# Zeros ahead of the first matmuls, held first loads, and a free place for the third weight chunk in a two-layer decoder trunk

## The chip, the cores and the metric

The kernel runs on one core of one Trainium2 chip. The time is device microseconds of one execution of the whole program. In three runs the kernel before took 571.51 to 573.66 us, median 572.7 us.

## What is computed

A trunk of two decoder layers over 256 tokens of width 1024, all in float32. Layer 0 mixes tokens with a gated MLP over chunks of 128 positions, layer 1 with causal attention over 16 heads. Each layer then has a gated MLP of width 2816 with a causal convolution of width 3. Every sub-layer ends in a layer norm of `alpha * x + f(x)`. The change touches the first product of all, the `v` half of `x @ w_in`:

```python
def chunked_gmlp(x, w_in, ln_g, ln_b, w_s, b_s, w_out):
    z = jax.nn.gelu(x @ w_in)
    u, v = jnp.split(z, 2, axis=-1)
    v = layer_norm(v, ln_g, ln_b)
    ...
    sv = jnp.einsum('gts,bnsgc->bntgc', w, v) + b_s.T[None, None, :, :, None]
    return (u * sv.reshape(B, S, GMLP_WIDTH)) @ w_out

def reference(x, ...):
    for i in range(DEPTH):
        ...
        x = layer_norm(DN_ALPHA * x + y, ln_mix_g[i], ln_mix_b[i])
        y = conv_ffn(x, f_w_up[i], f_conv_w[i], f_conv_b[i], f_w_down[i])
        x = layer_norm(DN_ALPHA * x + y, ln_ffn_g[i], ln_ffn_b[i])
    return x
```

## The kernel before

**Products in three parts.** Each float32 operand is split into a rounded part (`hi`, type float32r) and the rest (`lo`), and a product is the sum of three TensorE products, hi·hi, hi·lo and lo·hi. `split` (L357) makes the two parts: the hi copy on ScalarE through `act` (L338) or on VectorE (L361), the lo subtraction on VectorE through `tt` (L344). All matmuls are issued by `mms` (L326), all loads by `load` (L355) on SyncE's queue.

**The weight stream.** All weights come as a stream of chunks of 128 x 2048 values, 1 MiB each (`stream`, L367). `prep(i)` (L385) loads chunk i into one of two `raw` tiles and splits it into two `sub` pairs of 128 x 1024, taken from a ring of ten `whi` and ten `wlo` tiles (five chunks). Chunks 0 to 4 are prepared at the start, each later one when the chunk five before it is used up (`spent`, L409). A `raw` tile is free again when both subs of its chunk have been split, so chunk 2 shares its tile with chunk 0 and chunk 3 with chunk 1.

**The order.** Operations are recorded first, with a cost each, and `Plan.emit` then gives every engine a fixed order by those costs and by due times. The nine first loads have a fixed rank instead, called load 0 to load 8 here: load 0 is columns 0 to 511 of chunk 0, load 2 columns 512 to 1023, load 4 columns 1024 to 2047 (`FIRST`, L382); load 6 and load 7 are the halves of chunk 1; loads 1, 3, 5 and 8 bring the transposed input `xT` for k = 0, k = 1, k = 2 and 3, and k = 4 to 7 (`XFIRST`, L383). After them SyncE's queue holds chunk 2, chunk 3, the layer norm's rows (`lnrow`), chunks 4 and 5, `wsT`, `bs`, and later ones.

**The first product** (`gmlp`, L641). Four PSUM banks hold the sums of two halves of the tokens (t = 0, 1) by two halves of the 1024 columns. Chunk c carries the rows of k = 2c (its first sub) and k = 2c + 1 (its second). A step (k, t) is six matmuls of 128 x 512, three for each column half (`rows_step`, L553). The order is k = 0 to 3 with both t, then k = 4 to 7 for t = 0, then k = 4 to 7 for t = 1: 16 steps, 96 matmuls. Within a column half the order is hi·hi, then input hi by weight lo, then input lo by weight hi. After it come GELU, layer norm and the `u` half (chunks 4 to 7).

**Space.** `ff` is a tile of 6144 columns whose parts are handed out by `place` (L251). At the start `xT` lies in columns 512 to 2559; columns 2560 to 4607 are idle until `wsT` (from 3072), `bs` (from 4096) and parts of `u` are placed there.

Of the kernel before, what the change touches and what calls it, by code (L numbers as in the profile page):

```python
# [18 lines left out]
P = 128  # L19
D = 1024  # L20
# [25 lines left out]
T1_WAITS = (2600, 3300, 4000, 4700)  # L46
REST = 25000, 9000, 25000
AHEAD = 12000


class Buf:
# [172 lines left out]
def trunk_kernel(ctx: ExitStack, tc: tile.TileContext, a: dict, out: bass.AP):  # L224
# [48 lines left out]
    banks += [b[:, o:o + HALF] for o in (0, HALF) for b in twos]  # L273
    ALONE, BY_TWO = range(BANKS // 2), range(BANKS // 2, BANKS)
    bank_of = [(i - BANKS, None, False) for i in range(BANKS)]
    state = {"age": 0, "next": 0}

    def taken(i, long):
        old = bank_of[i][1]
# [34 lines left out]
                bank_of[i] = (bank_of[i][0], b, False)  # L314


    def mms(seq, r, w, fill=False):

        ns = 0.0
        for o, l, x, _, _ in seq:  # L320
            n = flat(x)
            ns += max(107.0, n / 2.4) + 2.5 if l.dtype == F32R else (218.0 if n <= P else n / 0.6 + 5)

        def emit():
            for o, l, x, start, stop in seq:
                nc.tensor.matmul(o, l, x, start=start, stop=stop)  # L326
        plan.op("pe", ns, emit, r, w, fill)

# [21 lines left out]
    def ts(o, x, s1, s2, op0, op1, r, w):  # L350
        dve(187 + 0.52 * flat(x), lambda: nc.vector.tensor_scalar(o, x, s1, s2, op0=op0, op1=op1), r, w)

    def load(o, src, w, r=(), nbytes=None, rank=None):
        nbytes = nbytes or flat(o) * P * 4
        plan.op("sp", nbytes / 360.0, lambda: nc.sync.dma_start(o, src), r, w, nbytes=nbytes, rank=rank)  # L355

    def split(hi, lo, src, psum=False, by="act"):  # L357

# [21 lines left out]


    FIRST = {0: [(0, 512, 0), (512, 1024, 2), (1024, 2048, 4)], 1: [(0, 1024, 6), (1024, 2048, 7)]}  # L382
    XFIRST = ((0, 1, 1), (1, 1, 3), (2, 2, 5), (4, 4, 8))  # L383

    def prep(i):  # L385
        name, c = stream[i]
        raw = raws.new()
        cuts = FIRST.get(i, [(0, CH, None)])
        for s, e, rank in cuts:
            load(raw.ap[:, s:e], a[name][c, :, s:e], [(raw, range(s // 256, e // 256))], rank=rank)  # L390
        subs = []
        for s in range(2):
            hi, lo = whi.new(), wlo.new()
            pieces = [(0, 512), (512, 1024)] if i in FIRST or i in FINE else [(0, SUB)]
            for b, e in pieces:
                src = raw.ap[:, s * SUB + b:s * SUB + e]
                split((hi, range(b // 256, e // 256), hi.ap[:, b:e]), (lo, range(b // 256, e // 256), lo.ap[:, b:e]),
                      (raw, range((s * SUB + b) // 256, (s * SUB + e) // 256), src))
            subs.append((hi, lo))
        chunks[i] = subs  # L400
# [27 lines left out]

    xh, xl = xt_new()
    xT32 = place("ff", HALF, KT * S)  # L430
    xv32 = xT32.ap.rearrange("p (t k c) -> p t k c", t=NT, k=KT)

    def load_xt(k, n, rank):
        load(xv32[:, :, k:k + n, :], a["xT"][:, :, k:k + n, :], [(xT32, [(t, j) for t in range(NT) for j in range(k, k + n)])],
             rank=rank)
        for t in range(NT):
            parts = [(t, j) for j in range(k, k + n)]
            split((xh, parts, xt_view(xh)[:, t, k:k + n, :]), (xl, parts, xt_view(xl)[:, t, k:k + n, :]),
                  (xT32, parts, xv32[:, t, k:k + n, :]), by="dve" if k == 0 else "act")
# [9 lines left out]
    def ln_rows(i):  # L449
        b = rowring.new()  # L450
        src = a["lnrow"]
        load(b.ap, bass.AP(tensor=src.tensor, offset=src.offset + i * 2 * D, ap=[[0, P], [1, 2 * D]]), [b])
        return b, b.ap.rearrange("p (a d) -> p a d", a=2)

    def load_mixer():
# [94 lines left out]
            plan.later(wait, lambda k0=k0: turn(k0))  # L550


    def rows_step(pieces, hk, lk, r, hi, lo, first, last):  # L553

        for o, n, b in pieces:
            parts = range(o // 256, (o + n) // 256)
            mms([(b.ap[:, :n], x, w.ap[:, o:o + n], first and j == 0, last and j == 2)
                 for j, (x, w) in enumerate([(hk, hi), (hk, lo), (lk, hi)])], r + [(hi, parts), (lo, parts)], [b])
        plan.tick()

    def cols_times(b, h, l, hi, lo):
# [79 lines left out]
    def gmlp():  # L641
        at = xt_at(xh, xl)
        pieces = [[(o, HALF, bank(True)) for o in (0, HALF)] for _ in range(NT)]
        order = [(k, t) for k in range(4) for t in range(NT)] + [(k, t) for t in range(NT) for k in range(4, KT)]
        v = []
        for k, t in order:
            rows_step(pieces[t], *at(k, t), *sub("a_v", k // 2, k % 2), k == 0, k == KT - 1)
            if t == NT - 1 and k % 2:
                spent("a_v", k // 2)
            if (k, t) == (3, NT - 1):  # L650
                rows = ln_rows(0)
                ws, bs = load_mixer()
            if k == KT - 1:
                vt = place("ff", HALF + t * D, D)
                for o, n, b in pieces[t]:
                    act(vt.ap[:, o:o + n], b.ap, AF.Gelu_apprx_tanh, [b], [(vt, range(o // S, (o + n) // S))],
                        psum=True, table="gelu")
                    done_with(b)
                st, mean, rstd = stats(vt, vt.ap, [(0, HALF), (HALF, HALF)])
                scaled(vt, vt.ap, st, mean, rstd, rows)  # L660
                v.append(vt)
# [226 lines left out]
    at = conv_up(1, h, l)  # L888
    project_out("f_dn1", FT, at, xtok, None, 4)
    plan.tick(1e9)  # L890
    plan.emit()


# [9 lines left out]
def _layout(i):  # L903
# [10 lines left out]
    def paired(wa, wb):  # L914
# [3 lines left out]
    w_in, qkv = np.asarray(i["a_w_in"])[0], np.asarray(i["b_w_qkv"])[0]  # L918
    g = {
        "x": f(x.reshape(NT, P, D).transpose(1, 0, 2)),  # L920
        "xT": f(x.reshape(NT, P, KT, P).transpose(3, 0, 2, 1)),
        "a_v": by_rows(w_in[:, D:]),
        "a_u": f(tiles(w_in[:, :D]).reshape(4, 2, P, SUB).transpose(0, 2, 1, 3).reshape(4, P, CH)),
        "a_out": by_rows(np.asarray(i["a_w_out"])[0]),
# [45 lines left out]
```

## Time and profile before

| what | value |
|---|---|
| median of three runs | 572.7 us (571.51 to 573.66) |
| the profiled execution | 571.2 us |
| its span, first to last instruction | 569.5 us |
| mean granted TensorE clock | 0.995 |
| moved by DMA | 110.92 MB, mean 195 GB/s |

The span stands 1.7 us below the profiled execution's own time and 3.2 us below the median of the three runs. PE is TensorE's matmuls, PEld its weight loads, DVE VectorE, ACT ScalarE, POOL GpSimd, and SPq SyncE's queue, which issues the loads; L and a number is a line of the kernel. In a row of the timeline the first number is the start in us, the second the time that the group took, and the bracket the idle time of the engine before it, with what ended it.

### The profile page before, as it was taken

To read this page: it belongs to the slowest core of one execution; us is meant where nothing else is said; L and a number is where in the kernel's file an instruction comes from. 1 tells how busy PE (TensorE), PEld (TensorE's weight loads), DVE (VectorE), ACT (ScalarE), POOL (GpSimd) and SP (SyncE) were. 2 spreads that over 40 slices of the span, in tenths; PEclk is the share of its full clock that TensorE was granted. 3 is DMA by queue.
4 is the path that set the end of the run, shared out by engine and by line. 5 is a ranking of instruction groups with operands and counts; after the bars stand their busy time and mean duration, and the time that the engine had idled before them with its cause. 6 is when DMAs were issued, how large, how long until landed. Compare 5 with 4: busy or idle time off the path is not lost.

```text
span 569.5 us, 8289 instructions
## 1 busy us (share of the span) xinstructions
PE 556.1 (98%) x3098; PEld 474.9 (83%) x3098; DVE 464.3 (82%) x873; ACT 359.2 (63%) x652; POOL 11.5 (2%) x17
## 2 busy tenths in 40 slices
PE   6999999999999999999999999999999999999994
PEld 4799888888888878888888877788888888888884
DVE  5598989999999997467958988579989999996526
ACT  5555558776777686335578877377777767775300
POOL 0020010000000000001000000010000000000001
PEclk9999999999999999999999999999999999999998
DMA  7897435547554577742665653506455556566302
GB/s 266 330 361 283 181 146 182 189 153 279 171 211 155 216 229 266 270 165 74 222 221 185 194 210 115 222 2 221 156 218 219 201 174 218 195 242 229 147 1 74
DMA packets 20132, 110.92 MB, mean 195 GB/s; under 512 B 2251, under 2 KB 6268, under 8 KB 7676
## 3 DMA queue, kind: packets, MB, share of 16 engines
q1 hardware_dynamic: 20092, 110.39, 54.2%
q8 instruction: 24, 0.39, 0.3%
q14 instruction: 16, 0.13, 0.1%
HBM read 109.31 MB, written 1.07 MB: 194 GB/s over the span
## 4 chain that ended last, share of the span: by engine, by line
PE 95%; DMA 2%; DVE 1%; SPq 0%; ACT 0%; issue 0%; DVEq 0%
PE twos L326 52%; PE bank L326 41%; DMA raw<-in_a_v 2%; PE bank L332 1%; PE twos L332 1%; DVE wlo L344 0%; DVE x L348 0%; SPq L355 0%; ACT whi L338 0%; DVE stat L494 0%; DVEq L966 0%; DVE stat L497 0%; DVE stat L499 0%; DVE xt L344 0%
## 5 line engine op out<-in xcount | busy, mean ns | idle before, releaser
L344 DVE TENSOR_TENSOR wlo<-raw,whi 128x1024 fp32r<-128x1024 f32 (+1 forms) x212 | 228.2, 1099 | 33.7 <-ACT whi L338 32.8
L338 ACT ACTIVATE whi<-raw 128x1024 fp32r<-128x1024 f32 (+1 forms) x212 | 194.8, 954 | 55.1 <-DMA raw<-in_f_dn 21.3
L326 PE MATMUL twos<-xt,whi 128*128 128x512 f32 x640 | 222.2, 394 | 0.0
L326 PE MATMUL twos<-xt,wlo 128*128 128x256 f32 x640 | 177.3, 277 | 0.0
L326 PEld LDWEIGHTS twos<-xt,whi 128*128 128x128 f32 x640 | 120.0, 188 | 27.8
L326 PE MATMUL bank<-whi,rr 128*128 128x512 f32 x432 | 135.5, 391 | 0.0
L326 PEld LDWEIGHTS twos<-xt,wlo 128*128 128x128 f32 x640 | 120.1, 188 | 0.1
L326 PEld LDWEIGHTS bank<-whi,rr 128*128 128x128 f32 x432 | 81.1, 188 | 17.9 <-issue 1.0
L326 PE MATMUL bank<-wlo,rr 128*128 128x512 f32 x216 | 84.0, 389 | 0.0
L326 PE MATMUL bank<-xt,whi 128*128 128x256 f32 (+1 forms) x256 | 71.0, 348 | 0.0
L348 DVE SCALAR_TENSOR_TENSOR ff<-ff,convc 128x254 f32<-128x254 f32 (+1 forms) x160 | 69.6, 478 | 0.3
L338 ACT ACTIVATE ff<-twos 128x512 f32<-128x512 f32 (+1 forms) x56 | 30.8, 565 | 47.9 <-PE twos L326 44.8
L326 PE MATMUL bank<-xt,wlo 128*128 128x256 f32 x192 | 54.0, 281 | 0.0
L326 PEld LDWEIGHTS bank<-xt,whi 128*128 128x128 f32 x256 | 44.0, 190 | 6.8 <-issue 1.0
L326 PEld LDWEIGHTS bank<-wlo,rr 128*128 128x128 f32 x216 | 40.6, 188 | 8.0
L338 ACT ACTIVATE ff<-ff,convc 128x256 f32<-128x256 f32 x80 | 45.6, 592 | 1.9 <-DVE ff L344 1.2
L344 DVE TENSOR_TENSOR ff<-twos,ff 128x512 f32<-128x512 f32 (+1 forms) x48 | 30.9, 645 | 15.3 <-ACT ff L338 13.0
L326 PE MATMUL twos<-whi,xt 128*128 128x512 f32 x128 | 42.1, 396 | 0.0
L338 ACT ACTIVATE ff<-bank,lncol 128x128 f32<-128x128 f32 x48 | 18.8, 458 | 29.1 <-PE bank L332 29.1
L326 PEld LDWEIGHTS bank<-xt,wlo 128*128 128x128 f32 x192 | 36.4, 190 | 0.0
L348 DVE SCALAR_TENSOR_TENSOR x<-x,bank 128x512 f32<-128x512 f32 x16 | 11.0, 686 | 25.0 <-PE bank L326 25.0
L326 PEld LDWEIGHTS twos<-whi,xt 128*128 128x128 f32 x128 | 24.1, 188 | 4.8
(71 smaller groups left out, 489.1 us busy)
## 6 DMA issues: line engine op xcount, KB each, us to landing
raw<-in_f_up SPq DMA_DIRECT2D x44, 1024.0 KB, 4.8
raw<-in_f_dn SPq DMA_DIRECT2D x22, 1024.0 KB, 4.9
raw<-in_b_qk SPq DMA_DIRECT2D x8, 1024.0 KB, 4.9
lnrow<-in_lnrow SPq DMA_DIRECT2D x5, 1024.0 KB, 6.7
raw<-in_a_u SPq DMA_DIRECT2D x4, 1024.0 KB, 5.1
raw<-in_a_out SPq DMA_DIRECT2D x4, 1024.0 KB, 5.0
raw<-in_b_v SPq DMA_DIRECT2D x4, 1024.0 KB, 4.9
raw<-in_b_o SPq DMA_DIRECT2D x4, 1024.0 KB, 5.0
```

Source lines behind the costliest of these rows:

```text
L326: nc.tensor.matmul(o, l, x, start=start, stop=stop)
L332: nc.tensor.transpose(o, x, ident.ap)
L338: plan.op("act", ns, lambda: nc.scalar.activation(o, x, func, **kw), r, w, table=table)
L344: dve(70 + 1.04 * flat(x), lambda: nc.vector.tensor_tensor(o, x, y, op=op), r, w)
L348: lambda: nc.vector.scalar_tensor_tensor(o, x, s, y, op0=op0, op1=op1), r, w)
```

## The change

Five edits, all at the start of the program; the costs given to the planner stay as they are.

- Before everything that the planner ordered, VectorE sets 512 columns of the still unused tile `rr` to zero, and TensorE does eight matmuls of 128 x 512 on them into the last PSUM bank.
- Some loads are preceded on SyncE's queue by a transfer of 16 numbers that reads a place of an earlier chunk and so waits until that part of it has landed. Load 5 is so held by load 0, load 7 by load 4, the halves of chunk 2 by loads 6 and 7, the halves of chunk 3 by the halves of chunk 2, and the first `lnrow` by the first half of chunk 3.
- Chunk 2 goes to columns 2560 to 4607 of `ff`. Chunk 3 then takes the `raw` tile of chunk 0, chunk 4 that of chunk 1, and the later ones alternate as before. Chunks 2 and 3 are each loaded in two halves.
- `xT` lies in the order k, t, so that a load of n values of k is one run of n x 1024 bytes in each partition, where it was two runs of n x 512.
- The twelve matmuls of k = 0 are issued together, for each column half in the order hi·hi for both t, input lo by weight hi for both t, input hi by weight lo for both t.

```diff
+WARM = 8
...
-    def mms(seq, r, w, fill=False):
+    def mms(seq, r, w, fill=False, into=None, ready=False):
...
         def emit():
-            for o, l, x, start, stop in seq:
+            if into is not None and not ready:
+                return
+
+            for o, l, x, start, stop in seq if into is None else [q for _, _, q in sorted(into, key=lambda q: q[:2])]:
                 nc.tensor.matmul(o, l, x, start=start, stop=stop)
...
-    def load(o, src, w, r=(), nbytes=None, rank=None):
+    def load(o, src, w, r=(), nbytes=None, rank=None, holds=()):
...
+        n = flat(o) // max(1, len(holds))
+
+        def emit():
+            for j, (i, at) in enumerate(holds):
+                k = state["held"] = state["held"] + 16
+                nc.sync.dma_start(scratch[:, k:k + 16], loaded[i].ap[:1, at:at + 16])
+                if len(holds) > 1:
+                    nc.sync.dma_start(o[:, j * n:(j + 1) * n], src[:, j * n:(j + 1) * n])
+            if len(holds) < 2:
+                nc.sync.dma_start(o, src)
...
+    HOLD = {5: [(0, 0)], 7: [(0, SUB)], (2, 0): [(1, 0), (1, SUB)], (3, 0): [(2, 0), (2, SUB)]}
+    scratch = sb.tile([1, 128], F32, name="scratch")
+    loaded = {}
+    EARLY = 2
...
-        raw = raws.new()
+        raw = loaded[i] = raws.new()
+        if i == EARLY:
+
+            other = place("ff", HALF + KT * S, CH)
+            raw.ap, raw.prev = other.ap, raw.prev + other.prev
+            owners["ff"] = [(s, e, raw if b is other else b) for s, e, b in owners["ff"]]
+        elif i > EARLY:
+            raw.ap = raws.tiles[(i - 1) % RAWS]
...
-            load(raw.ap[:, s:e], a[name][c, :, s:e], [(raw, range(s // 256, e // 256))], rank=rank)
+            load(raw.ap[:, s:e], a[name][c, :, s:e], [(raw, range(s // 256, e // 256))], rank=rank,
+                 holds=HOLD.get(rank if rank is not None else (i, s), ()))
...
-    xv32 = xT32.ap.rearrange("p (t k c) -> p t k c", t=NT, k=KT)
+    xv32 = xT32.ap.rearrange("p (k t c) -> p t k c", t=NT, k=KT)
...
-        load(xv32[:, :, k:k + n, :], a["xT"][:, :, k:k + n, :], [(xT32, [(t, j) for t in range(NT) for j in range(k, k + n)])],
-             rank=rank)
+        sl = slice(k * S, (k + n) * S)
+        load(xT32.ap[:, sl], a["xT"][:, sl], [(xT32, [(t, j) for t in range(NT) for j in range(k, k + n)])], rank=rank,
+             holds=HOLD.get(rank, ()))
...
-        load(b.ap, bass.AP(tensor=src.tensor, offset=src.offset + i * 2 * D, ap=[[0, P], [1, 2 * D]]), [b])
+        load(b.ap, bass.AP(tensor=src.tensor, offset=src.offset + i * 2 * D, ap=[[0, P], [1, 2 * D]]), [b],
+             holds=[(3, 0)] if i == 0 else ())
...
-    def rows_step(pieces, hk, lk, r, hi, lo, first, last):
-
-        for o, n, b in pieces:
+    def rows_step(pieces, hk, lk, r, hi, lo, first, last, into=None):
+
+
+        for i, (o, n, b) in enumerate(pieces):
             parts = range(o // 256, (o + n) // 256)
-            mms([(b.ap[:, :n], x, w.ap[:, o:o + n], first and j == 0, last and j == 2)
-                 for j, (x, w) in enumerate([(hk, hi), (hk, lo), (lk, hi)])], r + [(hi, parts), (lo, parts)], [b])
+            seq = [(b.ap[:, :n], x, w.ap[:, o:o + n], first and j == 0, last and j == 2)
+                   for j, (x, w) in enumerate([(hk, hi), (hk, lo), (lk, hi)])]
+            if into is not None:
+                into += [(i, (0, 2, 1)[j], q) for j, q in enumerate(seq)]
+            mms(seq, r + [(hi, parts), (lo, parts)], [b], into=into, ready=into is not None and len(into) == 12)
         plan.tick()
...
+        into = []
         for k, t in order:
-            rows_step(pieces[t], *at(k, t), *sub("a_v", k // 2, k % 2), k == 0, k == KT - 1)
+            rows_step(pieces[t], *at(k, t), *sub("a_v", k // 2, k % 2), k == 0, k == KT - 1, into if k == 0 else None)
...
     plan.tick(1e9)
+
+    zeros = rr[:, :HALF]
+    nc.vector.memset(zeros.bitcast(F32), 0.0)
+    for _ in range(WARM):
+        nc.tensor.matmul(banks[-1], zeros[:, :P], zeros, start=True, stop=True)
     plan.emit()
...
-        "xT": f(x.reshape(NT, P, KT, P).transpose(3, 0, 2, 1)),
+        "xT": f(x.reshape(NT, P, KT, P).transpose(3, 2, 0, 1).reshape(P, KT * S)),
```

More of the change, by code (lines that the diff above doesn't have):

```diff
@@ L275, in trunk_kernel @@
     bank_of = [(i - BANKS, None, False) for i in range(BANKS)]
-    state = {"age": 0, "next": 0}
+    state = {"age": 0, "held": -16}
     def taken(i, long):
@@ L351, in ts @@
         dve(187 + 0.52 * flat(x), lambda: nc.vector.tensor_scalar(o, x, s1, s2, op0=op0, op1=op1), r, w)
-    def load(o, src, w, r=(), nbytes=None, rank=None):
+    def load(o, src, w, r=(), nbytes=None, rank=None, holds=()):
         nbytes = nbytes or flat(o) * P * 4
-        plan.op("sp", nbytes / 360.0, lambda: nc.sync.dma_start(o, src), r, w, nbytes=nbytes, rank=rank)
+        n = flat(o) // max(1, len(holds))
[7 more added lines that the diff above has]
+                nc.sync.dma_start(o, src)
+        plan.op("sp", nbytes / 360.0, emit, r, w, nbytes=nbytes, rank=rank)
     def split(hi, lo, src, psum=False, by="act"):
```

## The prediction, made before the changed kernel was run

> **What bounds the kernel now.** I began with the page's busy times and the chain that ended last:
>
> ```profile
> PE 556.1 (98%) x3098; PEld 474.9 (83%) x3098; DVE 464.3 (82%) x873; ACT 359.2 (63%) x652; POOL 11.5 (2%) x17
> ...
> PE 95%; DMA 2%; DVE 1%; SPq 0%; ACT 0%; issue 0%; DVEq 0%
> ```
>
> TensorE's matmuls carry 95% of the chain, so only time in which TensorE waits or runs slowly can go. The view of waits, asked for TensorE's matmuls over the whole span, has two rows:
>
> ```profile
> PE bank L326 <- DVE xt L361: 4.9, 1, 4.9
> PE bank L326 <- DVE wlo L344: 0.8, 1, 0.8
> ```
>
> Both belong to the first product. The chain in order of time shows what lies behind them:
>
> ```profile
> 3.15 5.63 DMA raw<-in_a_v
> 8.80 0.64 ACT whi L338
> ...
> 10.79 7.21 DMA raw<-in_a_v
> 18.03 1.07 ACT whi L338
> 19.12 1.24 DVE wlo L344
> 20.40 19.62 PE bank L326 x119
> ```
>
> Load 4 lands at 8.78. Its splits free raw tile 0, chunk 2 is issued at 10.79 and lands at 18.00, its splits take to 20.4, and from there the chain stays on TensorE. So I cut the first product into three windows (the columns are the stretch, its length, PE busy with matmuls counted, PEld busy likewise, granted clock, DMA share and GB/s) and looked at its matmuls in the timeline:
>
> ```profile
> 4.92:11.03 6.11, 6.03 (x14) 4.39 (x14) 1.00 0.90 308
> 11.03:20.40 9.37, 8.61 (x37) 6.57 (x36) 1.00 0.99 370
> 20.40:31.23 10.83, 10.83 (x48) 8.93 (x48) 1.00 0.87 323
> ...
> 4.92 0.77 PE L326 MATMUL bank<-whi,xt 128*128 128x512 f32 x1 [4.92 <-DVE xt L361]
> 5.77 0.80 PE L326 MATMUL bank<-wlo,xt 128*128 128x512 f32 x1
> ...
> 7.22 0.63 PE L326 MATMUL bank<-wlo,xt 128*128 128x512 f32 x1
> ...
> 8.50 0.63 PE L326 MATMUL bank<-wlo,xt 128*128 128x512 f32 x1
> ...
> 11.03 0.40 PE L326 MATMUL bank<-wlo,xt 128*128 128x512 f32 x1
> 11.26 0.40 PE L326 MATMUL bank<-whi,xt 128*128 128x512 f32 x1
> ```
>
> A window also counts the matmul that reaches into it, so 13, 36 and 47 start in the three, 96 in all. The last take 10.83 / 47 = 0.23 us each; between 7.22 and 8.50 three start, 0.43 each. The granted clock column reads 1.00 throughout, so the half rate, which ends at 11.03, shows in the spacing alone. At 0.23 the 96 would take 22.1 us, and they take 31.23 - 4.92 = 26.3. **These 4.2 us are all there is to gain** after the first matmul: 6.1 - 13 x 0.23 = 3.1 before 11.03, and 9.4 - 36 x 0.23 = 1.1 around the wait for chunk 2. The edits do nothing to the first load or its split, so the start stays.
>
> **The change part by part.** First the zeros and the new order of k = 0:
>
> ```profile
> 0.87 0.06 DVE L421 MEMSET nhalf<- 128x1 f32 x1 [0.87 <-PEq L963]
> ...
> 5.03 0.68 DVE L344 TENSOR_TENSOR wlo<-raw,whi 128x512 fp32r<-128x512 f32 x1
> 5.63 0.29 DVE L344 TENSOR_TENSOR xt<-ff,xt 128x128 fp32r<-128x128 f32 x1
> ```
>
> The memset of 128x512 has no row; it lies between 0.06 (one column) and 0.68 (a subtraction of its size). I take 0.4, since a fill reads nothing. It starts at 0.87, where VectorE has no other work until the input lands. Eight matmuls at 0.43 then run from 1.3 to 4.7, with a first latency of 0.77 to 5.0. They cost the path 0.1 us at most.
>
> What they buy: the rate rose 6.1 us after the first matmul, or 5.3 after the unbroken run from 5.77. Counted from 1.3, that is 6.6 to 7.4; I take 7.0. The new order starts with four matmuls that need no weight lo part (ready at 5.71), so the hole from 5.35 to 5.77 goes. From 5.0, five matmuls at 0.43 and seven at 0.23 end k = 0 at 8.8, against some 10.2 (12 matmuls) before. By "TensorE: Matmul & The Clock Gate" of the Trainium skill (Part 1, the HAM clock gate), the array runs at half rate until one free-running window of about 3.4 us was busy, so the phase varies. By that rule an estimate puts the rise anywhere from 4.7 to 8.1, and k = 0 would end from 8.0 to 9.3.
>
> Next the transfers: two windows with the columns of all five engines, the issue of load 5, the hi splits of load 6, and the times from issue to landing of load 0, of chunk 4 with nothing queued ahead, and of loads 6 and 7:
>
> ```profile
> 4.90:8.78 3.88, 3.78 (x8) 2.71 (x9) 2.21 (x7) 1.14 (x3) 0.00 (x0) 1.00 0.81 247
> 8.78:13.50 4.72, 4.72 (x17) 3.73 (x17) 3.83 (x7) 4.07 (x8) 0.00 (x0) 1.00 1.03 394
> ...
> 3.79 0.55 SPq L355 DMA_DIRECT2D ff<-in_xT  x1
> ...
> 10.96 1.16 ACT L338 ACTIVATE whi<-raw 128x512 fp32r<-128x512 f32 x2 [0.39 <-DMA raw<-in_a_v]
> ...
> L355 SPq DMA_DIRECT2D raw<-in_a_v x1: 384/384/384, 0.8 to 0.8; - x1
> ...
> DMA to landing us min/median/max: 3.4/3.4/3.4
> ...
> L355 SPq DMA_DIRECT2D raw<-in_a_u x1: 328/328/328, 21.5 to 21.5; - x1
> ...
> DMA to landing us min/median/max: 4.8/4.8/4.8
> ...
> L355 SPq DMA_DIRECT2D raw<-in_a_v x2: 432/516/600, 4.4 to 5.0; - x2
> ...
> DMA to landing us min/median/max: 6.6/6.9/7.2
> ```
>
> **Load 4.** Until 8.78 the engines are 81% busy for 247 GB/s, afterwards full for 394. The early stretch carries the xT loads in short rows, and the change doubles those rows. It also holds load 5 until load 0 has landed (0.8 + 3.4 = 4.2), plus one issue of about 0.55: out at 4.8 instead of 3.79. Unqueued, 512 KB would take between 3.4 (256 KB) and 4.8 (1 MB): 3.6, near the smaller, as 1 MB less 512 KB at 394 GB/s gives 3.5. So load 4, issued at 3.15, lands between 6.8 and 8.8; I take the middle, 7.8.
>
> **The holds.** A hold stops SyncE, and everything behind waits too: behind that of load 7 are load 8 and chunk 2, behind those of chunk 3 are `lnrow` and chunk 4. One step of a hold costs an issue, 0.55, and an unqueued landing, 3.6. So load 7 lands at 12.0 (before: 5.0 + 7.2 = 12.2), the second half of chunk 2 at 16.1 (before: 18.0) and of chunk 3 at 20.3. Load 6 lands near 9.6 (10.96 before). Chunk 2, which needs no tile now, goes out at 10.2 instead of 10.79; its first half lands, behind loads 7 and 8, near 14.5, and that of chunk 3 at 18.6. `wsT` and `bs`, which follow chunk 2 in its place, come after chunk 5 in the queue and find it split. The seven tiny transfers are counted by their issue; nobody waits for their data.
>
> **The sum.** A step cannot end before its last split. After load 4 come two splits on ScalarE and two on VectorE, which overlap, then eight matmuls: k = 1 ends at 7.8 + 3.8 = 11.6, or 8.8 + 12 x 0.23 = 11.6 by TensorE itself. k = 2 and 3 find their data ready and end at 17.1; chunk 2's lo part, split by 16.8, no longer stops anything. TensorE reaches k = 6 at 19.9 and needs its lo part at 20.1: 18.6 + 1.07 + 1.24 = 20.9, a new stall of 0.8. For k = 7 it is 20.3 + 2.3 = 22.6, with 29 matmuls from there: 22.6 + 6.7 = 29.3. **The first product ends at 29.3 instead of 31.2: 2.0 us gained, and chunk 3 is what is late next.** As TensorE waits nowhere later, the gain should be kept if the later loads move up too:
>
> ```profile
> 21.51 2.82 SPq L355 DMA_DIRECT2D raw<-in_a_u  x2
> ```
>
> Chunk 4, issued there now, needs only chunk 1's tile, free two splits after load 7, and comes after `lnrow` at some 19.7; chunk 5 waits for chunk 3's splits at 22.6, where it now goes at the end of this row, by 24.3. Were this cover gone, `u` would pay it one for one. The profiled execution of 571.2 us (span 569.5) becomes 569.2 (span 567.5). The three runs have their median 1.5 us above it, 572.7, from which I count: **570.7 us**.
>
> **The rivals.**
> - *Zeros open nothing.* The rate rises only after real matmuls, at 11.0. Then k = 0 ends near 10.0, k = 1 at 13.3, and the rest, covering chunk 3, at 29.9: gain 1.3, 571.4 us. For it speaks that no row shows matmuls on zeros, against it that those of the trace need no particular data.
> - *The holds only cost.* If transfers are served strictly in their order, those behind take nothing from load 4; only the longer rows help (8.5), and the end is 30.0: gain 1.2, 571.5 us. For it speaks that landings keep the order of issue. Against it speaks that 1.65 MB had moved by 8.78 (4.9 us at 136 GB/s, then 3.88 at 247), where loads 0 to 4 are 1.31:
>
> ```profile
> 0.00:4.90 4.90, 0.00 (x0) 0.01 (x1) 0.41 (x4) 1.91 (x2) 0.70 (x6) 1.00 0.45 136
> ```
>
> "DMA: Bandwidth & Descriptors" of the Trainium skill (Queues, rings and completion order) states this rule for each engine's ring; the trace bears out the order, but not that nothing behind moves early.
> - *The data are early.* If load 4 lands by 7 and a landing takes 3.0, TensorE alone bounds: 8.8 + 84 x 0.23 = 28.1, gain 3.1, 569.6 us. Against it: the 3.4 above, for a load of half the size, is already more.
> - *Slower: the holds put landings in series.* Before, loads overlap in the queue; now chunk 3's second half needs three in turn. If each takes the 7.2 of load 7 or chunk 2, it lands at 7.8 + 3 x 7.75 = 31.1, and the product ends 9.0 later, at 40.1: 8.9 us lost, 581.6 us. It turns slower when that half lands after 22.2, that is when a step, issue included, takes over 4.8, and by more than 0.5% from 5.8 on. Against it: those 7.2 contain the queue that the holds remove, and 1 MB unqueued took 4.8.
>
> **How the numbers follow.** Chances: the forecast 0.52, with its own range 569.6 to 571.6; zeros open nothing 0.08; holds only cost 0.12; early data 0.24; slower 0.04. The low end is the best case, 4.2 less 0.1, with 0.2 for the scatter of runs: 568.4. The high end is a step of about 4.75, where the gain is 0.1: 572.6. Beyond lie the slower rival and runs of unusual scatter. A measurement of this kernel tells about 0.5% from no change, 2.9 us, so 569.8 is the limit of faster. Early data falls below it for 0.20 of its 0.24, the forecast for 0.08 of its 0.52: faster 0.28, same 0.68, slower 0.04.
>
> **What would show it.** Right: eight matmuls on `rr` from 1.3; spacing 0.23 from about 7; no hole at 5.4; load 4 landed near 7.8; SyncE's holds at 8, 12 and 16; the wait near 20 on chunk 3 and no longer on chunk 2; the first matmul of 256 columns at 29.3. Wrong: half rate to 11; load 4 still at 8.8; chunk 3 past 22; a wait of TensorE after 32, where there is none now.

## The result, and the profile after

The changed kernel takes 577.42 us (median of six runs, 575.1 to 578.98); the kernel before took 571.91 us in the runs beside it. The ratio is 1.01, with a 95% interval of 1.0082 to 1.0117: **slower by 1%, 5.5 us**. The prediction said 570.7 us, with a range up to 572.6; the time lies beyond it, on the side to which it gave 0.04.

The profiled execution took 577.39 us with a span of 575.6 us, 6.1 above that of before. Its page shows first what TensorE's matmuls carry, then the chain by engine:

```profile
PE 560.8 (97%) x3106; PEld 475.3 (83%) x3106; DVE 465.7 (81%) x874; ACT 359.9 (63%) x652; POOL 11.4 (2%) x17
...
PE 86%; DMA 7%; DVE 3%; ACT 2%; issue 1%; SPq 1%; DVEq 0%
```

TensorE held 95% of the chain before and holds 86% now; 7% is DMA. The view of waits of TensorE's matmuls, over the whole span, says where:

```profile
PE bank L330 <- DVE wlo L348: 4.0, 6, 0.8
PE twos L932 <- DVE nhalf L451: 1.5, 1, 1.5
PE twos L330 <- DVE ff L352: 1.0, 1, 1.0
PE bank L330 <- ACT whi L342: 0.6, 3, 0.2
```

The second row is the start before the zeros. The other three, 5.6 us in ten waits, stand against one of 0.8 before; the 1.0 of the third row lies in the `u` half. ScalarE's rows in the timeline, with the hi splits of the halves of chunks 2 and 3 and of chunk 4, show that the loads are what is late:

```profile
16.70 1.06 ACT L342 ACTIVATE whi<-ff 128x1024 fp32r<-128x1024 f32 x1
19.19 1.06 ACT L342 ACTIVATE whi<-ff 128x1024 fp32r<-128x1024 f32 x1 [1.43 <-DMA ff<-in_a_v]
22.07 1.06 ACT L342 ACTIVATE whi<-raw 128x1024 fp32r<-128x1024 f32 x1 [1.82 <-DMA raw<-in_a_v]
24.94 1.06 ACT L342 ACTIVATE whi<-raw 128x1024 fp32r<-128x1024 f32 x1 [1.80 <-DMA raw<-in_a_v]
...
33.29 2.01 ACT L342 ACTIVATE whi<-raw 128x1024 fp32r<-128x1024 f32 x2 [4.62 <-DMA raw<-in_a_u]
```

Each split begins the moment its half lands. The second half of chunk 3 lands at 24.94; the prediction had 20.3. SyncE's queue shows why it went out so late (L366 are the tiny transfers, L368 the halves, L370 other loads):

```profile
7.77 0.51 SPq L366 DMA_DIRECT2D scratch<-raw  x1
8.33 0.58 SPq L370 DMA_DIRECT2D raw<-in_a_v  x1
...
11.42 0.58 SPq L368 DMA_DIRECT2D ff<-in_a_v  x1
13.60 0.50 SPq L366 DMA_DIRECT2D scratch<-raw  x1
14.15 0.58 SPq L368 DMA_DIRECT2D ff<-in_a_v  x1
16.69 0.50 SPq L366 DMA_DIRECT2D scratch<-ff  x1
17.30 0.53 SPq L368 DMA_DIRECT2D raw<-in_a_v  x1
19.19 0.50 SPq L366 DMA_DIRECT2D scratch<-ff  x1
19.79 0.53 SPq L368 DMA_DIRECT2D raw<-in_a_v  x1
22.07 0.50 SPq L366 DMA_DIRECT2D scratch<-raw  x1
22.62 0.58 SPq L370 DMA_DIRECT2D lnrow<-in_lnrow  x1
23.29 4.32 SPq L370 DMA_DIRECT2D raw<-in_a_u  x2
```

A tiny transfer goes out when the part that it reads has landed, so these rows are also a list of landings: load 4 at 7.77, load 7 at 13.60, the second halves of chunks 2 and 3 at 19.19 and 24.94. **Each link of that chain takes 5.6 to 5.8 us**, where 4.15 was forecast. A second chain (load 6, the first halves of chunks 2 and 3, `lnrow`) runs between its links. Chunk 4 goes out at 23.29 and lands at 33.3, behind `lnrow` and with chunk 5 after it.

The loss has two parts. Before, the first matmul of 256 columns, which ends the first product, started at 31.23. Here are that matmul and the next two waits, from TensorE's timeline of after:

```profile
34.41 0.50 PE L330 MATMUL bank<-xt,whi 128*128 128x256 f32 x2 [0.23 <-ACT whi L342]
...
35.67 0.39 PE L330 MATMUL bank<-xt,wlo 128*128 128x256 f32 x1 [0.76 <-DVE wlo L348]
...
45.59 0.94 PE L330 MATMUL twos<-ff 128*128 128x128 f32 x6 [1.04 <-DVE ff L352]
```

So 3.2 us are lost by 34.41 (0.23 of it is already a wait for chunk 4). The same stretch of 96 matmuls then begins at 61.70 in the chain of after and at 55.81 in that of before, one row of each:

```profile
61.70 19.86 PE bank L330 x96
```

```profile
55.81 19.86 PE bank L326 x96
```

That is 5.9: **3.2 us in the first product and 2.7 in the `u` half**. The second part is chunk 4. Its splits stand ahead of the layer norm's statistics in VectorE's fixed order. VectorE's timeline of after, and of before, at that place:

```profile
34.39 5.75 DVE L348 TENSOR_TENSOR wlo<-raw,whi 128x1024 fp32r<-128x1024 f32 x4 [4.99 <-ACT whi L342]
40.06 1.87 DVE L526 BATCH_NORM_STATS2 stat<-ff 128x6 f32<-128x512 f32 x3
```

```profile
30.27 2.36 DVE L344 TENSOR_TENSOR wlo<-raw,whi 128x1024 fp32r<-128x1024 f32 x2 [0.53 <-ACT whi L338]
32.55 1.87 DVE L494 BATCH_NORM_STATS2 stat<-ff 128x6 f32<-128x512 f32 x3
```

VectorE sits idle for 5 us, the statistics come 7.5 us later than before, and TensorE waits for the normalized `v` at 45.59. That the late chunk 4 is the cause of this part is read from these rows; the run without `lnrow`'s hold, below, bears it out.

### The profile page after: what moved, and what is told of

Its sections match the earlier page's. It is cut to its first block, busy times and chain, and to the rows that moved or that the text cites. A ratio compares the mean times of both kernels' runs of the same rounds, so it can differ in the third digit from the quotient of the medians.

```text
span 575.6 us, 8323 instructions
## 1 busy us (share of the span) xinstructions
PE 560.8 (97%) x3106; PEld 475.3 (83%) x3106; DVE 465.7 (81%) x874; ACT 359.9 (63%) x652; POOL 11.4 (2%) x17
## 4 chain that ended last, share of the span: by engine, by line
PE 86%; DMA 7%; DVE 3%; ACT 2%; issue 1%; SPq 1%; DVEq 0%
PE twos L330 51%; PE bank L330 33%; DMA raw<-in_a_u 3%; DMA raw<-in_b_o 2%; DMA raw<-in_a_v 2%; PE bank L336 1%; DMA ff<-in_xT 1%; ACT ff L342 1%; DVE wlo L348 1%; ACT whi L342 1%; PE twos L336 1%; SPq L370 0%; DVE x L352 0%; DVE ff L866 0%; DVE ff L875 0%
## 5 line engine op out<-in xcount | busy, mean ns | idle before, releaser
L342 ACT ACTIVATE ff<-bank,lncol 128x128 f32<-128x128 f32 x48 | 18.9, 459 | 29.2 <-PE bank L336 29.2
```

What stands on the lines that cost most here:

```text
L342: plan.op("act", ns, lambda: nc.scalar.activation(o, x, func, **kw), r, w, table=table)
```

## The experiments

Seventeen kernels ran. The table holds those made from the changed kernel; the times are medians over several runs, but the last three columns are read from one profiled execution each. Landings are taken from the start of the hi split that waits for them, and the last column is the start of the first matmul of 256 columns, so it can hold a wait for chunk 4 (0.2 us in the changed kernel, 1.3 with the tiny ones doubled).

| kernel | time, us | ratio to before (95%) | load 4 | end of chunk 3 | 256 columns |
|---|---|---|---|---|---|
| changed kernel | 577.42 | 1.01 (1.0082 to 1.0117) | 7.77 | 24.94 | 34.41 |
| no holds | 570.2 | 0.9971 (0.9953 to 0.9988) | 9.27 | 19.37 | 29.67 |
| `lnrow` not held | 577.35 | 1.0097 (1.0084 to 1.011) | 7.88 | 25.84 | 37.15 |
| chunks 2, 3 not held | 572.2 | 1.0002 (0.9986 to 1.0019) | 7.73 | by 19.9 | 29.36 |
| loads 5, 7 held only | 572.14 | 1.0005 (0.9987 to 1.0024) | 8.02 | 21.01 | 30.09 |
| load 5 held only | 569.95 | 0.9961 (0.9938 to 0.9984) | 7.82 | 19.93 | 29.92 |
| loads 5, 8 held only | 570.13 | 0.9966 (0.9948 to 0.9985) | 7.77 | 19.31 | 29.24 |
| chunk 3, `lnrow` not held | 572.96 | 1.0038 (1.0015 to 1.006) | 7.46 | 22.15 | 31.25 |
| tiny ones read `bs` | 571.55 | 0.9995 (0.9975 to 1.0015) | 10.29 | 20.33 | 32.27 |
| tiny ones doubled | 578.15 | 1.0117 (1.0083 to 1.0151) | 7.32 | 26.36 | 36.90 |
| `lnrow` after chunk 5 | 578.22 | 1.0111 (1.0079 to 1.0143) | 7.56 | 27.43 | 38.45 |
| no zeros | 576.48 | 1.0086 (1.0061 to 1.0112) | 7.78 | 23.83 | 32.91 |
| holds one earlier | 573.16 | 1.0023 (0.9999 to 1.0046) | 7.85 | 20.81 | 29.93 |
| one at a time (one run) | 586.74 | | 7.61 | 33.20 | 44.84 |

### Is it the holds?

All seven tiny transfers taken away, the halves, the free place and the zeros kept (a hold of `None` issues its half without a tiny transfer):

```diff
-    HOLD = {5: [(0, 0)], 7: [(0, SUB)], (2, 0): [(1, 0), (1, SUB)], (3, 0): [(2, 0), (2, SUB)]}
+    HOLD = {(2, 0): [(None, 0), (None, 0)], (3, 0): [(None, 0), (None, 0)]}
...
-             holds=[(3, 0)] if i == 0 else ())
+             holds=())
```

> The change without its seven tiny transfers; the free place, the halves, the zeros, the new order and the xT rows stay. Theory A (the holds put landings of about 5 us in series, and that alone costs): chunk 3 lands by 18 instead of 24.9, the waits of TensorE on chunks 2 and 3 go, the first product ends near 28, and the time is 567.5 to 569.5 us, under the kernel before. Rival B (the halves or the free place make the landings slow, the holds only show it): half chunks still take about 5 us each from issue, chunk 3 lands after 22, and the time stays above 574.

The time falls to 570.2 us, 0.3% below the kernel before: the whole loss hangs on the holds. The windows of after and then of this kernel (length, the busy times of the five engines, granted clock, DMA share, GB/s) show what they did to the transfers:

```profile
8.00:16.00 8.00, 7.77 (x32) 5.46 (x31) 4.64 (x8) 4.54 (x10) 0.00 (x0) 1.00 0.80 268
16.00:25.00 9.00, 6.54 (x23) 3.91 (x23) 4.97 (x5) 3.84 (x6) 0.00 (x0) 1.00 0.64 203
```

```profile
8.00:16.00 8.00, 6.75 (x29) 5.00 (x28) 5.60 (x10) 5.79 (x11) 0.00 (x0) 1.00 1.01 396
16.00:25.00 9.00, 9.00 (x42) 7.44 (x41) 5.75 (x6) 6.34 (x7) 0.00 (x0) 1.00 0.94 369
```

From 16 to 25 us the DMA engines move 203 GB/s with the holds and 369 without.

### The transfers or the waiting?

The tiny transfers read the input `bs`, which is always there, so they wait for no load's data:

```diff
-                nc.sync.dma_start(scratch[:, k:k + 16], loaded[i].ap[:1, at:at + 16])
+                nc.sync.dma_start(scratch[:, k:k + 16], a["bs"][:1, :16])
```

> All seven tiny transfers at their places, but each reads 16 numbers of an input in memory, so that it waits for no load. Theory A (the waiting costs, not the transfers): the issues cost 7 x 0.55 us of a queue that has time, the rest is as without holds, 569.5 to 571.5 us. Rival F (the tiny transfers themselves slow the loads behind them): half chunks still take about 5 us each in a row, and the time is over 574.

5.9 us of the time go with the waiting for the loads that were read. Not all waiting is gone: SyncE's waits still have 5.4 us in five waits of the tiny transfers and the halves for landings, and the first half of chunk 2 goes out at 10.28, when load 4 lands. What makes it wait there wasn't looked into. And the other way, each tiny transfer issued twice:

```diff
                 nc.sync.dma_start(scratch[:, k:k + 16], loaded[i].ap[:1, at:at + 16])
+                nc.sync.dma_start(scratch[:, 128 + k:128 + k + 16], loaded[i].ap[:1, at + 16:at + 32])
```

> The change with each tiny transfer doubled (the second reads the next 16 numbers, which have landed with the first). Theory A (only the waiting and the issue cost): each step grows by one issue, 0.55, four steps in a row to chunk 3: 2 to 3 us slower than the changed kernel, 579 to 581 us, with the landing of the halves unchanged at 4.8 to 5.3. Rival F (a tiny transfer slows the load behind it): landings grow to 6 and more, over 582.

The median is 0.7 us higher, less than expected. The links grow by the added issue, some 0.6 each, and the last half lands 1.4 later, at 26.36. The profiled execution, the slowest of the four, took 579.83 us, 2.4 above that of the changed kernel; with four runs from 576.82 to 579.83 and six from 575.1 to 578.98, a cost of 0.7 and one of 2 can't be told apart. That execution also ran at half rate from 38.2 to 41.4 (granted clock 0.51), which the changed kernel's did not.

### Which hold?

Only `lnrow`'s hold removed:

```diff
-             holds=[(3, 0)] if i == 0 else ())
+             holds=())
```

> The change without the hold ahead of lnrow alone. Theory A says that this hold costs a second time, as it puts lnrow (1 MB) right in front of chunk 4: without it chunk 4 lands by 29 instead of 33.3, the wait at the start of the u half (about 1.0) and the one of the spatial matmuls (about 1.2) go, and the time falls by 1.5 to 3 us to 574.5 to 576. Rival C (chunk 4 is late only because chunk 3 was): no change, 577 to 578.

The loss only moves. `lnrow` and chunk 4 now go out at 19.35 and 19.88, right behind the last half of chunk 3, and that half takes 7.0 us instead of 5.1:

```profile
18.78 0.53 SPq L368 DMA_DIRECT2D raw<-in_a_v  x1
19.35 0.43 SPq L370 DMA_DIRECT2D lnrow<-in_lnrow  x1
19.88 8.63 SPq L370 DMA_DIRECT2D raw<-in_a_u  x2
```

The 256 columns start at 37.15, 2.7 later than with the hold. The landing, 25.84 against 24.94, accounts for 0.9 of that. The rest is TensorE's rate: it waited 2.0 us for that half, and then ran at half rate for 6 us. Here are two rows of its timeline, and a window with the columns as above, in which the granted clock reads 0.52:

```profile
26.95 0.80 PE L330 MATMUL bank<-whi,xt 128*128 128x512 f32 x1 [1.99 <-ACT whi L342]
...
28.80 1.06 PE L330 MATMUL bank<-whi,xt 128*128 128x512 f32 x2
...
27.00:33.20 6.20, 5.74 (x13) 4.23 (x14) 3.24 (x4) 4.27 (x5) 0.00 (x0) 0.52 0.79 289
```

Chunk 4 lands at 30.72 here, and the `u` half loses nothing: from 37.15 to the stretch of 96 matmuls, at 61.73, are 24.6 us, as from 31.23 to 55.81 before. In the changed kernel they are 27.3. The same with `lnrow` issued unheld after chunk 5, so that chunk 4 goes out without it:

```diff
-            if len(holds) < 2:
+            if wait:
+                state["wait"] = (o, src)
+            elif len(holds) < 2:
                 nc.sync.dma_start(o, src)
+            if then:
+                nc.sync.dma_start(*state["wait"])
...
-                 holds=HOLD.get(rank if rank is not None else (i, s), ()))
+                 holds=HOLD.get(rank if rank is not None else (i, s), ()), then=i == 5)
...
-             holds=[(3, 0)] if i == 0 else ())
+             wait=i == 0)
```

> The change with the first lnrow load not held but issued after chunk 5; all other holds stay. If the part of the loss behind the first product (5.9 in all less 3.2 at its end) comes from lnrow standing in front of chunk 4, chunk 4 lands by 27 instead of 33.3, and the time is 574 to 575.5 us. If it is only the late chunk 3: 577 to 578.

My expectation failed for the same reason: chunk 4 goes out at 20.61, behind the half issued at 19.98, which lands 7.45 us after its issue, and a wait of 2.4 us is again followed by half rate. So the cure isn't in what follows the holds. Next, the holds of the chunks removed, those of loads 5 and 7 and of `lnrow` kept:

```diff
-    HOLD = {5: [(0, 0)], 7: [(0, SUB)], (2, 0): [(1, 0), (1, SUB)], (3, 0): [(2, 0), (2, SUB)]}
+    HOLD = {5: [(0, 0)], 7: [(0, SUB)], (2, 0): [(None, 0), (None, 0)], (3, 0): [(None, 0), (None, 0)]}
```

> The change without the four tiny transfers of chunks 2 and 3; loads 5, 7 and lnrow stay held. Theory A: the halves go out at 10 to 11 and land by 14.5 to 18, lnrow goes at about 17, and the time is 568.5 to 570.5 us. Rival D (the holds of loads 5 and 7 already delay everything behind them): chunk 3 lands after 20 and the time is 571.5 or more.

The loss is gone, but there is no gain: `lnrow`'s hold leaves a hole in the transfers at 18.9 to 20.9, and chunk 4 lands at 26.76. With `lnrow` free too, so that only loads 5 and 7 are held:

```diff
-             holds=[(3, 0)] if i == 0 else ())
+             holds=())
```

> The change with the holds of loads 5 and 7 alone; chunks 2 and 3 and lnrow go out freely. Theory A, as the runs before left it: load 4 lands at 7.7, chunk 3 by 20, lnrow is out by 12 and chunk 4 lands by 26, so the hole in the transfers near 19 that the hold of lnrow left goes, and with it the late u half: 569 to 570.5 us. Rival C2 (with chunks 2 and 3 unheld, lnrow's hold is harmless, the loss lies elsewhere): 571.5 to 573.

Still no gain (1.0005), so the hole wasn't all. The first product ends at 30.09, but in the `u` half TensorE waits 1.5 us for `ff`, and chunk 5 lands at 31.08, where it lands at 28.24 with load 5 alone held. That kernel, below, takes 569.95 us, so holding load 7 costs some 2 us. And with chunk 2's holds back, chunk 3 and `lnrow` free:

```diff
-    HOLD = {5: [(0, 0)], 7: [(0, SUB)], (2, 0): [(None, 0), (None, 0)], (3, 0): [(None, 0), (None, 0)]}
+    HOLD = {5: [(0, 0)], 7: [(0, SUB)], (2, 0): [(1, 0), (1, SUB)], (3, 0): [(None, 0), (None, 0)]}
```

> The change with the holds of loads 5 and 7 and of chunk 2's halves; chunk 3 and lnrow are free. Theory A: chunk 3's halves go out with chunk 2's second half, near 14.7, land by 19 to 20.5, and the first product does not wait for them: 571.5 to 573 us, so that most of the loss hangs on the last two steps of the series. If each step of the series costs alike: 574.5 to 575.5.

1.0038: of the 5.5 us, 4.5 hang on the holds of chunk 3 and `lnrow`, and the second half of chunk 3 lands at 22.15, just at the 22.2 that the prediction had named as the point of no gain.

### Which hold helps?

Load 5's alone kept:

```diff
-    HOLD = {5: [(0, 0)], 7: [(0, SUB)], (2, 0): [(1, 0), (1, SUB)], (3, 0): [(2, 0), (2, SUB)]}
+    HOLD = {5: [(0, 0)], (2, 0): [(None, 0), (None, 0)], (3, 0): [(None, 0), (None, 0)]}
...
-             holds=[(3, 0)] if i == 0 else ())
+             holds=())
```

> The change with the hold of load 5 alone. If a hold pays only where the transfer behind it would take from one that TensorE waits for, load 4 lands between 7.7 (loads 5 and 7 held) and 9.3 (nothing held), near 8.3, and load 8 lands by 13 instead of 14.9: 568.5 to 570 us. If any hold is a loss, more than the 570.2 of the run without holds.

0.9961, below both kernels (the interval ends at 0.9984). The splits of load 4 and the last half, in ScalarE's timeline of this kernel:

```profile
7.82 1.15 ACT L342 ACTIVATE whi<-raw 128x512 fp32r<-128x512 f32 x2 [0.57 <-DMA raw<-in_a_v]
...
19.93 1.06 ACT L342 ACTIVATE whi<-raw 128x1024 fp32r<-128x1024 f32 x1 [0.20 <-DMA raw<-in_a_v]
```

Load 4 lands at 7.82 where it landed at 9.27 without holds, though it was issued at 2.65 in both: what is issued behind it does take from it. With load 8 held until load 4 has landed as well:

```diff
-    HOLD = {5: [(0, 0)], (2, 0): [(None, 0), (None, 0)], (3, 0): [(None, 0), (None, 0)]}
+    HOLD = {5: [(0, 0)], 8: [(0, SUB)], (2, 0): [(None, 0), (None, 0)], (3, 0): [(None, 0), (None, 0)]}
```

> The change with load 5 held by load 0 and load 8 held by load 4, load 7, the chunks and lnrow free. If a hold pays only for the load that TensorE waits for next: load 4 lands near 7.8, load 6 by 11, load 8 by 15, the first product ends at 28.8 to 29.5, and the time is 568.5 to 570 us. If the bus must stay full above all: chunk 2 is late again as with loads 5 and 7 held, 571 to 572.5 us.

0.9966, with the intervals of the two and of the kernel without holds overlapping: which of these three is best can't be told.

### The zeros

The kernel before with the memset and the eight matmuls alone, and the changed kernel without the matmuls:

```diff
+WARM = 8
...
+    zeros = rr[:, :HALF]
+    nc.vector.memset(zeros.bitcast(F32), 0.0)
+    for _ in range(WARM):
+        nc.tensor.matmul(banks[-1], zeros[:, :P], zeros, start=True, stop=True)
```

```diff
-WARM = 8
+WARM = 0
```

> The kernel before with the eight matmuls on zeros alone. Theory A: full rate from about 5, but the first product still waits for chunk 2 until 20.4, so all that is gained goes into a longer wait: 571.4 to 572.4 us, no change. Rival E (the clock's start counts by itself): 2.5 to 3 us faster, 569 to 569.5.

> The change without the zeros (no matmul on them; the memset stays). Theory A: the waits on chunks 2 and 3 come after, and swallow what the clock's late start costs: 577 to 578.5 us, no change against the changed kernel. Rival E: 2.5 to 3 us more, 580 to 580.5.

Alone they bring nothing (572.52 us, 1.0009, 0.9997 to 1.002), though the matmuls do reach 0.23 us each soon after 5 us: TensorE then waits for splits, 1.6 us in all, most of it for load 4 and chunk 2. In the profiled execution 1.3 us are still gained at the first matmul of 256 columns (29.95), 0.7 at the stretch of 96 (55.11) and none over the span (569.6); where the rest goes wasn't followed. The changed kernel without them takes 576.48 us, 0.9 less than with them, which the two intervals don't tell from nothing. That TensorE only waits longer for the halves after an early start fits this, and isn't shown by it.

### Why does a link take 5.6 us?

First, what a half costs by itself. Chunks 4, 14 and some later ones in halves in the kernel before, nothing held:

```diff
+    HALVES = {i: [(0, SUB, None), (SUB, CH, None)] for i in (4, 14, 16, 18, 20, 22, 24, 26, 28)}
...
         cuts = FIRST.get(i, [(0, CH, None)])
+        cuts = HALVES.get(i, cuts)
```

> The kernel before, with chunks 4 and 14, 16, ... 28 loaded in two halves and nothing held: a measurement of the landing of 512 KB with nothing, or nothing but its own second half, in the queue. The forecast took 3.6 us. If 3.4 to 3.8 is measured, what made the held halves land in 4.8 to 5.3 is what stood with them in the queue (the tiny transfer ahead, the other half); if 4.5 or more, a landing hardly depends on the size, and the forecast's price was wrong by itself.

The one run took 572.57 us. A half with nothing else under way lands in 3.6 us. This is the answer for chunk 14's, in the view by tile:

```profile
L355 SPq DMA_DIRECT2D raw<-in_f_up x2: 328/328/328, 67.7 to 71.6; - x2
...
DMA to landing us min/median/max: 3.6/3.6/3.6
```

So the term of the prediction holds for what it names, and does not describe the links. Then one tiny transfer, released by a split, right ahead of a half:

```diff
+            if ahead is not None:
+                k = state["next"] = state["next"] + 16
+                nc.sync.dma_start(scratch[:, k:k + 16], chunks[ahead - 2][0][1].ap[:1, :16].bitcast(F32))
             nc.sync.dma_start(o, src)
```

> The kernel before, with every second chunk from 12 on in two halves, and a tiny transfer of 16 numbers right ahead of the first half of every fourth chunk, released by the same split as the half. Where the queue is empty, a half without it lands in 3.6 us as measured. Rival F (the tiny transfer holds up the load behind it): 4.6 to 5.2 behind a tiny transfer, which by itself explains the held halves. Theory G (what is in flight beside a half holds it up): 3.5 to 3.9 behind a tiny transfer too.

The seven such halves issued from 59 to 203 us took 3.8 to 5.0, most of them 4.2 or 4.3, and an eighth, at 218, took 6.1: between the two theories, with another chunk still under way beside several of them. That settled nothing (the one run took 571.77 us). Next the second half of every fourth chunk held until the first has landed, as in the changed kernel:

```diff
-                nc.sync.dma_start(scratch[:, k:k + 16], chunks[ahead - 2][0][1].ap[:1, :16].bitcast(F32))
+                nc.sync.dma_start(scratch[:, k:k + 16], ahead.ap[:1, :16])
```

> The kernel before, every second chunk from chunk 12 on in two halves; on every fourth chunk (16, 20, 24, 28, ...) the second half is held, by one tiny transfer, until the first half has landed; nothing at the start is changed. Open is why a half takes 4.8 to 5.3 us in the series of the changed kernel, when a half alone takes 3.6 and one behind a tiny transfer that reads older data took 3.8 to 5.0, mostly 4.2. Rival H (it is the series itself: a half that goes out right on the landing of the half before it): the held second halves take 4.6 to 5.3 here too. Rival I (it is the place, the start of the program with its other loads): they take 3.6 to 4.2 here, like a half behind any tiny transfer. Either way the time stays within 1 us of the kernel before, as these loads have slack.

The held halves of the up product land in 3.8 to 4.1, six of six (the first of the down product in 4.7); one row and its landing:

```profile
L360 SPq DMA_DIRECT2D raw<-in_f_up x1: 521/521/521, 88.8 to 88.8; - x1
...
DMA to landing us min/median/max: 3.8/3.8/3.8
```

So a hold in itself makes no landing long. The other half of the expectation failed: the one run took 578.12 us. From 200 us on, in the down product, the chain went through the landings of `f_dn`, and TensorE waited 3.8 us for `x` after it; there, in this one execution, the loads have no slack.

What was left is what the start has and these places have not: a second chain of halves. The holds laid so that one transfer at a time is under way:

```diff
-    HOLD = {5: [(0, 0)], 7: [(0, SUB)], (2, 0): [(1, 0), (1, SUB)], (3, 0): [(2, 0), (2, SUB)]}
+    HOLD = {5: [(0, 0)], 7: [(1, 0)], (2, 0): [(1, SUB), (2, 0)], (3, 0): [(2, SUB), (3, 0)]}
...
-             holds=[(3, 0)] if i == 0 else ())
+             holds=[(3, SUB)] if i == 0 else ())
```

> The changed kernel with the holds of load 7, of the halves of chunks 2 and 3 and of lnrow each looking at the transfer right before (load 7 waits for load 6, the halves of chunk 2 for load 7 and for each other, those of chunk 3 likewise, lnrow for the last half), so that one chain of landings takes the place of two that interleave. Rival J (a half is slowed by the half of the other chain that is under way with it): the held halves of chunks 2 and 3 land 3.6 to 4.2 us after their issue, as the held second halves did later in the program, the tiny ones in 1.6 to 2. Rival K (it is the place): they take 4.8 to 5.3 as in the changed kernel. In both cases more steps stand in series, the last half lands past 29, and the time is 578 to 588.

The issues in the DMA view, with KB each and the median from issue to landing, of after (10 to 26 us) and of this kernel (15 to 34 us):

```profile
ff<-in_a_v SPq DMA_DIRECT2D x2, 512.0 KB, 5.3
raw<-in_a_v SPq DMA_DIRECT2D x2, 512.0 KB, 4.9
...
scratch<-raw SPq DMA_DIRECT2D x3, 0.1 KB, 3.3
```

```profile
ff<-in_a_v SPq DMA_DIRECT2D x2, 512.0 KB, 3.9
raw<-in_a_v SPq DMA_DIRECT2D x2, 512.0 KB, 3.8
...
scratch<-raw SPq DMA_DIRECT2D x3, 0.1 KB, 1.6
```

That settles it for the other chain and against the place: the same halves, at the same place, land in 3.8 and 3.9 us alone and in 4.9 to 5.3 beside the half of the other chain; the tiny ones in 1.6 and in 3.3. Of the 1.5 us by which a link missed its forecast, some 0.3 is the half behind its hold (3.85 against 3.6) and 1.2 the other chain. More links in series cost more all the same: the last half lands at 33.20 and the one run takes 586.74 us. Some 2.6 us of that are again the rate: 33.20 + 2.3 + 29 x 0.23 is 42.2, the 256 columns start at 44.84, and the granted clock reads 0.50 from 27.5 to 41.0.

Last, the opposite: each hold but load 5's looks one transfer further back.

```diff
-    HOLD = {5: [(0, 0)], 7: [(0, SUB)], (2, 0): [(1, 0), (1, SUB)], (3, 0): [(2, 0), (2, SUB)]}
+    HOLD = {5: [(0, 0)], 7: [(0, 512)], (2, 0): [(0, SUB), (1, 0)], (3, 0): [(1, SUB), (2, 0)]}
...
-             holds=[(3, 0)] if i == 0 else ())
+             holds=[(2, SUB)] if i == 0 else ())
```

> The changed kernel with every hold but that of load 5 looking one transfer further back (load 7 waits for load 2, the halves of chunk 2 for loads 4 and 6, those of chunk 3 for load 7 and the first half of chunk 2, lnrow for the second half of chunk 2), so that two transfers are under way at a time; the seven tiny transfers and all waits stay in kind. Theory A (the series leaves the memory idle between landings): the second half of chunk 3 lands at 19 to 21 instead of 24.9, TensorE waits under 1 us for it, the time is 569.5 to 572.5. Rival (each held step costs its 5 us whatever else is under way, or the holds cost by their number): chunk 3 lands past 23 and the time stays at 574 or more.

With as many tiny transfers and as many waits, the last half lands at 20.81, TensorE waits 0.4 us for splits in the first product, and 4.3 of the 5.5 us come back (573.16, 0.7 above the range that I gave). A half takes 5.1 us here too, but more of them are under way at a time: from 16 to 25 us it moves 338 GB/s, at a DMA share of 0.94. What does not come back lies in the `u` half: in the profiled execution (573.59 us) the 256 columns start 1.3 us earlier than in the kernel before, but then TensorE waits 1.7 us for `ff`, and it runs at half rate after it:

```profile
41.60:44.90 3.30, 3.30 (x19) 3.30 (x18) 3.30 (x5) 0.93 (x2) 0.00 (x0) 0.51 1.02 379
```

## Why the prediction was wrong, step by step

**What bounds the kernel** held: from the stretch of 96 matmuls on, TensorE takes 513.9 us (575.6 - 61.7) where it took 513.7 (569.5 - 55.8), so all that moved, moved before 62 us.

**Zeros and the order of k = 0: right, and better than forecast.** The rows of TensorE's start in after:

```profile
1.51 3.78 PE L932 MATMUL twos<-rr 128*128 128x512 f32 x8 [1.51 <-DVE nhalf L451]
5.09 1.45 PE L330 MATMUL bank<-whi,xt 128*128 128x512 f32 x4
6.38 0.62 PE L330 MATMUL bank<-wlo,xt 128*128 128x512 f32 x2
6.86 1.20 PE L330 MATMUL bank<-whi,xt 128*128 128x512 f32 x4
7.89 0.62 PE L330 MATMUL bank<-wlo,xt 128*128 128x512 f32 x2
```

A pair takes 0.62 at 6.38, the full rate, where 7.0 was forecast for the rise and 8.8 for the end of k = 0, which comes at 8.5. The rise, between 5.1 and 6.4, is in the early half of the range, 4.7 to 8.1, that the prediction estimated from the Trainium skill's "TensorE: Matmul & The Clock Gate" (Part 1, the HAM clock gate), and matmuls on zeros open the gate: the rival against it is out.

**Load 4: right**, 7.77 against 7.8. The exact hit is luck, as 7.8 was the middle of 6.8 to 8.8; the twelve kernels that hold load 5 read 7.32 to 8.02. What holding load 5 does was judged rightly too. "DMA: Bandwidth & Descriptors" of the Trainium skill (Queues, rings and completion order) has each ring consumed in order, though a later descriptor may finish its write first; here load 4 lands at 9.27 with everything issued behind it and at 7.8 with load 5 held, so order alone does not keep what follows from slowing an earlier transfer of this queue, and "the holds only cost" is out as well. Nor do the longer rows show a gain by themselves: that 9.27 compares with 8.80 before. (Against this rival the prediction also counted 1.65 MB moved by 8.78; its own terms make 1.62, which changes nothing.)

**The holds: the step that failed.** "One step of a hold costs an issue, 0.55, and an unqueued landing, 3.6." The second term was mis-sized: the landing measured 5.0 to 5.3, with 0.55 to 0.6 of issue 5.6 to 5.8 a link. The word that failed is *unqueued*. The plan itself listed two chains, loads 4, 7 and the second halves, and load 6 and the first halves, each with its own times; that a half of the one is under way beside a half of the other stood in those times and wasn't priced in the chain that mattered. Three links at 5.7 instead of 4.15 make the 4.6 us between 20.3 and 24.94.

**The end of the first product.** From there the working holds: 24.94 + 2.3 for the splits + 29 matmuls at 0.23 is 33.9, and 34.41 was measured, 0.23 of the difference a wait for chunk 4.

**The cover of chunk 4: named, and not carried into the slower case.** "Were this cover gone, `u` would pay it one for one": chunk 4 landed at 33.3 where the kernel before had it at 26.3 (21.51 + 4.8), and the `u` half paid 2.7 us. The slower rival counted the first product alone, so at a landing of 25 us it gave a loss of 2.7 and not the 5.5 of the runs.

**The rival and its chance.** *The holds put landings in series* was the right mechanism, with the right place and the right point of decision: half of chunk 3 at 22.2, a link of 4.8. Its price of 7.2 a landing, 7.75 a link, was too high, as that held a longer queue. The mistake was to set one value, 4.15, against one other, 7.75, with 4.75 as the end of the range, and to call everything beyond 4 in 100. The rows had given only these two ends, and 4.8 lies nearer to the lower; a third or so for the slower side would have been a fairer judgement.

**The gain that was forecast can be had, but not by this working.** With load 5's hold alone the time is 569.95 us, 2.0 below the 571.91 of the kernel before, and TensorE waits nowhere after the first product. But the 256 columns start at 29.92 there, a gain of 1.3 and not 2.0, the interval allows 0.9 to 3.5 us, and six of the seven holds are gone. That the size agrees is partly luck.

## What to carry to other kernels

A hold that lets a critical transfer land first is worth its price once, on the load right behind it; a chain of holds turns a stream that is limited by bandwidth into one that is limited by landing time, and the bytes under way divided by the landing tell what is left of the rate (one half per 2.84 us is 185 GB/s here, against 369 to 396 without holds). Price a link with everything that is under way beside it, the plan's own other transfers first. And follow a delayed load through the fixed orders behind it: here the splits of a late chunk held up the layer norm, which cost nearly as much as the product that waited for the load. Last, look at the clock after each new wait of TensorE: in seven of these kernels a wait was paid twice, once as idle time and once as half rate behind it.

## What the runs showed of the hardware

- Transfers issued later on the same queue lengthen those ahead of them, though landings kept the order of issue: load 4 takes 6.6 us from issue to landing with all behind it, 5.1 with load 5 held; the last half of chunk 3 takes 5.1 in the changed kernel, 7.0 with `lnrow` and chunk 4 right behind, 7.45 with chunk 4.
- 512 KB land 3.6 us after their issue with an idle queue and 1 MB after 4.8, so that the second half MB adds 1.2 us. A straight line through the two leaves some 2.4 us for no byte, an estimate that does not reach down to the smallest sizes (64 bytes took 1.6). The Trainium skill's "DMA: Bandwidth & Descriptors" (Anatomy of one DMA — SWDGE (gpsimd) path) has a fixed 2.0 us for another path of issue; by that estimate the loads here have such a cost too, a little above that size. A chain of holds pays it at every link.
- A transfer of 64 bytes lands in 1.6 us alone and in 2.7 to 3.3 behind a half of 512 KB on the same queue (4.7 with a second one under way): the four issued from 13.60 on landed 0.1 to 0.2 us after the half ahead of them.
- At the start the clock in the profile's rows read 1.00 whether the matmuls ran at 0.43 or 0.23 us each, so what the zeros open shows in the spacing only. Later it does show: behind new waits of TensorE it read 0.50 to 0.54, over 6 us with `lnrow` not held (a wait of 2.0), from 12.7 to 16.4 with the tiny ones reading `bs` (2.6), and over 3.3 us with the holds one earlier (1.0). The wait of 1.0 at 45.59 in the changed kernel was not followed by it (1.00 from 45 to 55), so the length of a wait alone does not settle it.
